# Encoder trunk on one core: later turns and two more products ahead of gate/up, grid transfers spread over attention units

## The chip, the cores and the metric

One Trainium2 chip, one NeuronCore of it. The metric is the device time of one execution in microseconds (us). The engines are named as the profile names them: PE is TensorE (PEld its weight loads), DVE VectorE, ACT ScalarE, POOL GpSimd, SP SyncE, which issues every DMA of this kernel; "SPq" is its queue.

## What is computed

Two transformer layers on 1024 tokens of width 1024, all float32. Layer 0 mixes tokens by windowed attention (12 heads, window of 128 to each side, T5 bias, sink), layer 1 by attention over a 16 x 64 grid of tokens (8 x 16 neighbourhood, relative bias). Four heads of each layer attend to a memory of 256 rows. Then a SwiGLU feed-forward layer:

```python
h = rms_norm(x, norm_mix_pre[i])
tok = windowed_gqa(...) if i % 2 == 0 else neighbourhood_attn(...)
mixed = concatenate([tok, mem_out]) @ w_out[i]
x = x + rms_norm(mixed, norm_mix_post[i])
h = rms_norm(x, norm_ffn_pre[i])
gu = h @ w_gu[i]                      # 1024 x 5632
f = (silu(gu[:, :2816]) * gu[:, 2816:]) @ w_down[i]
x = x + rms_norm(f, norm_ffn_post[i])
```

## The kernel before

**Products of float32.** Each operand is split into a high part (`fp32r`, ScalarE, L115, L918 or L1063) and a low part (the difference, VectorE or POOL, L116, L920 or L1064). A product is three matmuls: high x high, low x high, high x low (`mm3`, L91 to L93).

**Attention of a layer** (`heads`) runs over eight groups: six pairs of heads (0 to 5) and two pairs of memory heads (6, 7), in the order 0, 6, 1, 7, 2, 3, 4, 5. A group has 16 units (eight blocks of 128 query rows by two heads). For each unit PE computes scores (L254, L255), transposes probabilities (L282) three units later and weighs values (L292) five units later; between these the projection of the next group's queries is fed in evenly. Queries come in two halves of 512 columns. Where the two heads aren't set apart by the engines, `q_tiles` makes the high part (L208) and the low part (L209, `ql`) and three DMA moves (L201) put them into place; PE needs the moves of a half before the half's first scores.

**The grid bias of layer 1** is prepared in layer 0's attention by DMAs alone (`grid_tables`): 8 transfers fill two tables in DRAM from masks, 16 and 16 copy rows of the bias (rpb_d), and 16 and 8 copy from those to `bias_d`, all issued at L372. They are five lists; `group(p).units()` of a windowed pair takes one list and issues it in full, so the pairs 0, 1, 2, 3, 4 have them (L734). `keep_in_program_order` pins each issue behind what was emitted just before it on SP's queue.

**The output projection** runs over eight tiles of 128 tokens. After the matmuls of tile i, tile i - 1 is turned: `turn_tile` transposes its normed rows on PE (L186), ScalarE copies them to `z` (L838) and splits some into B11, B21, B22 (L97, L98). `tail` is the norm of a tile: two squares on ScalarE (L431), `ms` on VectorE (L161), `r` by POOL's power (L165), the scaling (L436), the sum with x (L437), a second square (L176), `ms` (L163), `r` again, and `ht` (L178), which the turn reads. From tile 4 on `combine` makes four differences (L853) on POOL, those of the last on VectorE, which are the operands T1 to T4.

**Gate/up** is a Strassen-Winograd product of 2 x 2 blocks: 22 iterations, f = 0, 11, 1, 12, ..., each of seven products of twelve matmuls (`product`). `A11 x B11` and `A12 x B21` need only tiles 0 to 3; the other five need T2, T1, T3, T4 and B22 and so all tiles, with the weight sums S1 to S4 (`Sums`, L954 to L957) and A22, split by `piece` (`gh` on ScalarE, `gl` on VectorE). Ahead of the T blocks the kernel computes the two products of gates 0, FH (11) and 1; the third gate's two stay in PSUM (`kept`) until iteration 2. Raw weights pass through a ring of two slots (`wr`), split gates through one of three (`wh`, `wl`).

**What sets the order.** Within attention PE's order is the program's. Elsewhere a planner places each instruction on its engine's queue by its own estimates of when it is ready, with the program's order as priority; engines then work their queues in order. `high_priority(offset=-60)` puts the query splits and moves 60 places back.

Of the kernel before, what the change touches and what calls it, by code (L numbers as in the profile page):

```python
# [66 lines left out]
def build(nc, tc, ctx, x_in, mem_in, wts, t5, onehot, sinks, rpb, maskb, gains, out):  # L67
# [43 lines left out]
    low = [nc.gpsimd]  # L111

    def split_raw(u, raw, pl, n, tiles=None, pin=False):
        h, lo = tiles or unit_tiles(u, pl, n)
        a = nc.scalar.activation(h, raw, AF.Copy)  # L115
        b = low[0].tensor_tensor(lo, raw, h.bitcast(F32), ALU.subtract)  # L116
        if pin:
            tc.keep_in_program_order(a)
            tc.keep_in_program_order(b)
        return h, lo  # L120
# [52 lines left out]
    def norm_rows(npool, xt, g, nb):  # L173
# [4 lines left out]
        nc.vector.scalar_tensor_tensor(ht, xt, r, g, ALU.mult, ALU.mult)  # L178
        return ht

# [59 lines left out]
    class Unit:  # L240


        def __init__(self, pair, j, hh, lo, nk, bias, sink, k):
            self.pair, self.j, self.hh, self.lo, self.nk = pair, j, hh, lo, nk
            self.bias, self.sink, self.k = bias, sink, k

# [54 lines left out]
    def heads(at2, groups):  # L301
# [29 lines left out]
        for units, its in groups:  # L331
# [3 lines left out]
            for n, u in enumerate(units):  # L335
                for part in range(2):
                    if part == 0:
                        u.scores(at2)
# [281 lines left out]
    for layer in range(DEPTH):  # L620
# [86 lines left out]
        if windowed:  # L707
# [12 lines left out]

            def group(p, order=order):
# [9 lines left out]
                def units():  # L731
                    if p < 5:
                        bias_tiles(p + 1)
                    for step in grid_todo.pop(0) if grid_todo else []:  # L734
                        step()
                    if p == order[2]:
                        mem_back(1)
                    return units_of(pr, bias, PAIRS_A[p])
# [45 lines left out]
        for m in range(2):  # L784
            pr = pair_of(6 + m, lambda m=m: mks[m], lambda b: mvs[b], 2 * m)
            units_by[6 + m] = lambda pr=pr: units_of(pr, None, None)
# [108 lines left out]
        for i in range(NT):  # L895
# [11 lines left out]
            if prev is not None:  # L907
                turn_tile(i - 1, prev)
            prev = tail(npool, i, accs, gpost, gpre, xt, x_new, False, 3)
# [5 lines left out]

        def piece(src):
# [3 lines left out]
            nc.vector.tensor_tensor(lo, src, h.bitcast(F32), ALU.subtract)  # L920
            return h, lo

        def product(A, B):
            acc = psO.tile([P, HALF], F32, name="acc", tag="acc")
# [115 lines left out]
        A = Sums(0, gates[0], spare.pop, nc.gpsimd)  # L1040
        gates.append(gate_unit(FH))
        for gate in gates:
# [6 lines left out]
        gates.append(gate_unit(1))  # L1049
        A11, A12 = ([t[:, k * HALF:(k + 1) * HALF] for t in gates[2][1]] for k in range(2))  # L1050
        kept = [product(A11, B11), product(A12, B21)]
        A.all()
        turn_tile(NT - 1, prev)
# [3 lines left out]
        T2, T1, T3, T4 = (block(cB, f"T{k}") for k in (2, 1, 3, 4))  # L1057
# [9 lines left out]
        for n in range(NF):  # L1067
            f = n // 2 + n % 2 * FH
            if n:
                gate = gates[n] if n < 3 else gate_unit(f)  # L1070
                if n == 2:
# [4 lines left out]
            else:  # L1076
                p1 = c11 = tmp("e")
                nc.scalar.activation(p1, kept.pop(0) if n == 2 else product(A.A11, B11), AF.Copy)
            act_sums(f, *gate_up(f, A, p1, c11, kept.pop(0) if n == 2 else None))
# [250 lines left out]
```

## Time and profile before

| | us |
|---|---|
| median of 3 runs (2249.93 to 2253.44) | 2252.22 |
| the profiled execution | 2251.45 |
| its span, first to last instruction | 2249.6 |
| PE busy in the span | 2143.0 |
| DVE busy | 1511.8 |
| ACT busy | 1063.4 |
| POOL busy | 718.9 |

Mean granted clock of PE over the span: 0.983. PE's matmuls are pipelined, so its busy time overlaps from one to the next. Layer 0's attention ends near 350 us, its projection near 448; gate/up of layer 0 follows until some 900 us, the down projection until some 1128; layer 1 repeats this, with its projection ending near 1574.

### The profile page before, as it was taken

To read this page: it belongs to the slowest core of one execution; us is meant where nothing else is said; L and a number is where in the kernel's file an instruction comes from. 1 tells how busy PE (TensorE), PEld (TensorE's weight loads), DVE (VectorE), ACT (ScalarE), POOL (GpSimd) and SP (SyncE) were. 2 spreads that over 40 slices of the span, in tenths; PEclk is the share of its full clock that TensorE was granted. 3 is DMA by queue.
4 is the path that set the end of the run, shared out by engine and by line. 5 is a ranking of instruction groups with operands and counts; after the bars stand their busy time and mean duration, and the time that the engine had idled before them with its cause. 6 is when DMAs were issued, how large, how long until landed. Compare 5 with 4: busy or idle time off the path is not lost.

```text
span 2249.6 us, 31265 instructions
## 1 busy us (share of the span) xinstructions
PE 2143.0 (95%) x10538; PEld 1781.7 (79%) x10538; DVE 1511.8 (67%) x2637; ACT 1063.4 (47%) x2162; POOL 718.9 (32%) x806
## 2 busy tenths in 40 slices
PE   7899898989999999999999999999899999999997
PEld 7678787768888888887788899778688888887875
DVE  5578785588777775557757665765887777755555
ACT  5488785453233332534457665754423333324333
POOL 3167661424333231102215342524233333310011
PEclk9999999999999999999999999999999999999999
DMA  6433445325555543866433222432245555437664
GB/s 207 119 87 94 126 145 148 108 75 178 183 178 173 176 157 122 286 200 225 149 107 97 78 78 74 137 113 102 74 176 184 179 174 174 163 118 276 197 200 146
DMA packets 153335, 336.49 MB, mean 150 GB/s; under 512 B 24759, under 2 KB 47159, under 8 KB 153176
## 3 DMA queue, kind: packets, MB, share of 16 engines
q1 hardware_dynamic: 153176, 334.50, 46.5%
q8 instruction: 84, 1.38, 0.3%
q14 instruction: 75, 0.61, 0.1%
HBM read 229.06 MB, written 95.03 MB: 144 GB/s over the span
## 4 chain that ended last, share of the span: by engine, by line
PE 72%; DVE 6%; ACT 5%; issue 5%; DMA 4%; POOL 3%; SPq 1%; POOLq 0%; DVEq 0%; ACTq 0%
PE acc L92 18%; PE acc L91 18%; PE acc L93 18%; PE psg L91 3%; PE psg L92 3%; PE psg L93 3%; PE psv L292 2%; PE pst L282 2%; PE pss L254 1%; PE pss L255 1%; POOL zh L853 1%; ACT sn L272 1%; DMA draw<-both_d 1%; DMA wr<-in_wts 1%; DMA draw<-in_wts 1%
## 5 line engine op out<-in xcount | busy, mean ns | idle before, releaser
L975 DVE TENSOR_TENSOR zt<-acc,zt 128x512 f32<-128x512 f32 x300 | 204.8, 686 | 155.4 <-PE acc L93 153.8
L274 POOL TENSOR_TENSOR sn<-sn,st 128x384 f32<-128x384 f32 (+1 forms) x256 | 188.2, 736 | 253.6 <-DVE st L273 219.1
L1120 DVE TENSOR_TENSOR dl<-draw,dh 128x1024 fp32r<-128x1024 f32 x119 | 148.5, 1257 | 133.6 <-ACT dh L1118 133.1
L1118 ACT ACTIVATE dh<-draw 128x1024 fp32r<-128x1024 f32 x119 | 125.3, 1058 | 172.9 <-PE acc L93 101.7
L92 PE MATMUL acc<-dl,dh 128*128 128x512 f32 x476 | 187.4, 394 | 8.8 <-DVE dl L1120 8.6
L91 PE MATMUL acc<-dh 128*128 128x512 f32 x476 | 186.2, 391 | 0.5 <-ACT dh L1118 0.5
L918 ACT ACTIVATE gh<-zt 128x512 fp32r<-128x512 f32 x168 | 104.4, 628 | 174.2 <-PE acc L92 155.4
L93 PE MATMUL acc<-dh,dl 128*128 128x512 f32 x476 | 185.9, 391 | 0.0
L994 POOL TENSOR_TENSOR tw<-tw 128x512 f32<-128x512 f32 x88 | 131.8, 1498 | 120.3 <-DMA tw<-in_wts 115.1
L116 DVE TENSOR_TENSOR wl<-wr,wh 128x1024 fp32r<-128x1024 f32 x92 | 120.1, 1306 | 68.5 <-ACT wh L115 66.9
L994 POOL TENSOR_TENSOR zt<-zt 128x512 f32<-128x512 f32 x66 | 90.4, 1370 | 205.1 <-DVE zt L972 201.6
L971 ACT ACTIVATE zt<-zt 128x512 f32<-128x512 f32 x84 | 53.1, 632 | 217.5 <-DVE zt L975 217.5
L91 PE MATMUL psg<-hH,wh 128*128 128x512 f32 x384 | 153.5, 400 | 1.8 <-DVE k L229 1.4
L115 ACT ACTIVATE wh<-wr 128x1024 fp32r<-128x1024 f32 x100 | 105.5, 1055 | 100.6 <-DMA wr<-in_wts 79.8
L92 PE MATMUL psg<-hL,wh 128*128 128x512 f32 x384 | 152.9, 398 | 0.0
L93 PE MATMUL psg<-hH,wl 128*128 128x512 f32 x384 | 152.7, 398 | 0.0
L1175 POOL TENSOR_TENSOR tt<-tt,g 128x512 f32<-128x512 f32 x28 | 45.8, 1652 | 334.3 <-ACT junk L1174 334.3
L292 PE MATMUL psv<-PT,v 128*128 128x256 f32 x656 | 143.1, 319 | 4.6 <-DVE attn L667 3.2
L98 DVE TENSOR_TENSOR PT<-pst,PT 128x384 fp32r<-128x384 f32 (+1 forms) x256 | 126.6, 495 | 29.2 <-ACT PT L97 24.6
L272 ACT ACTIVATE sn<-sn,st 128x385 f32<-128x385 f32 (+3 forms) x192 | 112.9, 588 | 61.8 <-DVE st L269 57.2
L920 DVE TENSOR_TENSOR gl<-zt,gh 128x512 fp32r<-128x512 f32 x168 | 129.6, 773 | 7.8 <-ACT gh L918 7.8
L282 PE MATMUL pst<-ident,sn 128*128 128x128 f32 x656 | 116.2, 277 | 8.2 <-POOL sn L274 4.5
(233 smaller groups left out, 6146.5 us busy)
## 6 DMA issues: line engine op xcount, KB each, us to landing
wr<-in_wts SPq DMA_DIRECT2D x146, 512.0 KB
draw<-both_d SPq DMA_DIRECT2D x88, 512.0 KB
both_d<-zt SPq DMA_DIRECT2D x88, 256.0 KB
tw<-in_wts SPq DMA_DIRECT2D x44, 512.0 KB
both_d<-tw SPq DMA_DIRECT2D x44, 512.0 KB
act_d<-zt SPq DMA_DIRECT2D x66, 256.0 KB
draw<-act_d SPq DMA_DIRECT2D x66, 256.0 KB
draw<-in_wts SPq DMA_DIRECT2D x66, 256.0 KB
```

The lines of the kernel that those rows point to most:

```text
L91: nc.tensor.matmul(ps, lh, rh, start=start, stop=False)
L92: nc.tensor.matmul(ps, lh, rl, start=False, stop=False)
L93: nc.tensor.matmul(ps, ll, rh, start=False, stop=stop)
L98: nc.vector.tensor_tensor(ol, ps, oh.bitcast(F32), ALU.subtract)
L272: nc.scalar.activation(sn[:, :m], sn[:, :m], AF.Exp, bias=nm, scale=-1.0, accum_out=ssum)
L274: nc.gpsimd.tensor_tensor(sf, sf, rinv.broadcast_to([P, n]), ALU.mult)
L282: nc.tensor.transpose(pt[:, c], self.sn[:, c * P:(c + 1) * P], ident)
L292: nc.tensor.matmul(pv[:, j % 2], pair.v(self.lo + c)[:, pair.vh + hh], self.PT[:, c], start=c == 0, stop=c == nk - 1)
L920: nc.vector.tensor_tensor(lo, src, h.bitcast(F32), ALU.subtract)
L975: nc.vector.tensor_tensor(o, a, b, ALU.add)
L994: nc.gpsimd.tensor_tensor(o, a, b, ALU.subtract)
L1120: eng.tensor_tensor(lo, raw, h.bitcast(F32), ALU.subtract)
```

## The change

In layer 0's attention each list of grid transfers is taken by a group, memory groups too, so the groups 0, 6, 1, 7, 2 have them; the n-th of its transfers is issued at the start of unit 1 + 14 n / length. Ahead of gate/up, tile 6 is turned after gate 0's two products and tile 7 after gate FH's two; the weight sums of f = 0 are made on VectorE in place of POOL, A22 is split at once, and the low parts of the other four sums are queued behind the last norm's `ht` and gate 1's low part (`late`). The products of gate FH + 1 are computed ahead as well, into the two PSUM banks of the turns, and used in iteration 3, for which the raw gate weights are loaded again. The T blocks are laid out in the reverse order. The diff:

```diff
@@ -109,11 +109,12 @@
         return [pl.tile([P, 1024], F32R, name=f"w{k}{u}", tag=f"w{k}{tag}", bufs=n) for k in "hl"]
 
     low = [nc.gpsimd]
+    split = [None]
 
     def split_raw(u, raw, pl, n, tiles=None, pin=False):
         h, lo = tiles or unit_tiles(u, pl, n)
         a = nc.scalar.activation(h, raw, AF.Copy)
-        b = low[0].tensor_tensor(lo, raw, h.bitcast(F32), ALU.subtract)
+        b = split[0] = low[0].tensor_tensor(lo, raw, h.bitcast(F32), ALU.subtract)
         if pin:
             tc.keep_in_program_order(a)
             tc.keep_in_program_order(b)
@@ -175,8 +176,15 @@
         ss = npool.tile([P, 1], F32, name="ss", bufs=4)
         nc.scalar.activation(ht, xt, AF.Square, scale=ROOT, accum_out=ss)
         r = rms(npool, [ss])
-        nc.vector.scalar_tensor_tensor(ht, xt, r, g, ALU.mult, ALU.mult)
+        normed[0] = nc.vector.scalar_tensor_tensor(ht, xt, r, g, ALU.mult, ALU.mult)
         return ht
+
+    normed = [None]
+
+    def behind(ins, first):
+
+        tc.add_manual_dep(ins.ins, first.ins.name, mybir.DependencyInfo(
+            mybir.DependencyClass.NoSync, mybir.DependencyReason.DATA), reason="queued behind")
 
     def turn(pspool, tag, ht, put):
 
@@ -243,6 +251,7 @@
         def __init__(self, pair, j, hh, lo, nk, bias, sink, k):
             self.pair, self.j, self.hh, self.lo, self.nk = pair, j, hh, lo, nk
             self.bias, self.sink, self.k = bias, sink, k
+            self.begin = []
 
         def scores(self, at2):
             j, hh, nk = self.j, self.hh, self.nk
@@ -335,6 +344,8 @@
             for n, u in enumerate(units):
                 for part in range(2):
                     if part == 0:
+                        for step in u.begin:
+                            step()
                         u.scores(at2)
                         line.append(u)
                     else:
@@ -718,6 +729,12 @@
                 for hh in range(2):
                     biases[p, hh] = b[:, hh]
 
+            def with_steps(us):
+                steps = grid_todo.pop(0) if grid_todo else []
+                for n, step in enumerate(steps):
+                    us[1 + n * (len(us) - 2) // len(steps)].begin.append(step)
+                return us
+
             def group(p, order=order):
                 c = p // 3
                 pr = pair_of(p, lambda: kts[c], lambda b: vts[b], 2 * c)
@@ -731,11 +748,10 @@
                 def units():
                     if p < 5:
                         bias_tiles(p + 1)
-                    for step in grid_todo.pop(0) if grid_todo else []:
-                        step()
                     if p == order[2]:
                         mem_back(1)
-                    return units_of(pr, bias, PAIRS_A[p])
+                    us = units_of(pr, bias, PAIRS_A[p])
+                    return with_steps(us)
 
                 return units, [q_item(U_A + p, keep_q(p), p in (order[0], order[7]))]
 
@@ -783,7 +799,7 @@
             units_by[p], needs[p] = group(p)
         for m in range(2):
             pr = pair_of(6 + m, lambda m=m: mks[m], lambda b: mvs[b], 2 * m)
-            units_by[6 + m] = lambda pr=pr: units_of(pr, None, None)
+            units_by[6 + m] = lambda pr=pr, then=with_steps if windowed else list: then(units_of(pr, None, None))
             needs[6 + m] = [q_item(um + m, keep_q(6 + m), not windowed)]
         for it in needs[order[0]]:
             now(it)
@@ -904,24 +920,29 @@
                         ds = slice(dh * HALF, (dh + 1) * HALF)
                         mm3(accs[dh], aH[:, c], aL[:, c], h[:, ds], lo[:, ds],
                             c0 + c == 0, c0 + c == 7)
-            if prev is not None:
+            if prev is not None and i < NT - 1:
                 turn_tile(i - 1, prev)
-            prev = tail(npool, i, accs, gpost, gpre, xt, x_new, False, 3)
+            before, prev = prev, tail(npool, i, accs, gpost, gpre, xt, x_new, False, 3)
         oph.close()
 
 
         gph = Phase()
         gp = gph.open(sb(f"gu{layer}", side="left"))
+
+        late = []
 
         def piece(src):
             h = gp.tile([P, HALF], F32R, name="gh", tag="gh", bufs=5)
             nc.scalar.activation(h, src, AF.Copy)
             lo = gp.tile([P, HALF], F32R, name="gl", tag="gl", bufs=5)
-            nc.vector.tensor_tensor(lo, src, h.bitcast(F32), ALU.subtract)
+            b = nc.vector.tensor_tensor(lo, src, h.bitcast(F32), ALU.subtract)
+            for ins in late:
+                behind(b, ins)
             return h, lo
 
-        def product(A, B):
-            acc = psO.tile([P, HALF], F32, name="acc", tag="acc")
+        def product(A, B, acc=None):
+            if acc is None:
+                acc = psO.tile([P, HALF], F32, name="acc", tag="acc")
             for kc in range(4):
                 ks = slice(kc * P, (kc + 1) * P)
                 mm3(acc, A[0][:, ks], A[1][:, ks], B[0][:, kc], B[1][:, kc], kc == 0, kc == 3)
@@ -1037,24 +1058,39 @@
         spare = [stage.tile([P, S], F32, name="attn", tag="attn", bufs=2) for _ in range(2)]
         spare = [t[:, k * HALF:(k + 1) * HALF] for t in spare for k in range(2)]
         gates = [gate_unit(0)]
-        A = Sums(0, gates[0], spare.pop, nc.gpsimd)
+        A = Sums(0, gates[0], spare.pop, nc.vector)
+        A.A22
         gates.append(gate_unit(FH))
-        for gate in gates:
+        for gate in gates[:]:
             p1 = gp.tile([P, D], F32, name="p1", tag="tw", bufs=2)
             p1, c11 = p1[:, :HALF], p1[:, HALF:]
             A11, A12 = ([t[:, k * HALF:(k + 1) * HALF] for t in gate[1]] for k in range(2))
             nc.scalar.activation(p1, product(A11, B11), AF.Copy)
             add(c11, product(A12, B21), p1)
             ahead.append((p1, c11))
-        gates.append(gate_unit(1))
-        A11, A12 = ([t[:, k * HALF:(k + 1) * HALF] for t in gates[2][1]] for k in range(2))
-        kept = [product(A11, B11), product(A12, B21)]
-        A.all()
-        turn_tile(NT - 1, prev)
+            turn_tile(NT - 3 + len(ahead), before if len(ahead) == 1 else prev)
+            if len(ahead) == 1:
+                gates.append(gate_unit(1))
+                late[:] = normed[0], split[0]
+                A.all()
+                late.clear()
+
+        def first_two(f, make):
+            if f != 1:
+                gates.append(gate_unit(f))
+            A11, A12 = ([t[:, k * HALF:(k + 1) * HALF] for t in gates[-1][1]] for k in range(2))
+            kept.append([make(A11, B11), make(A12, B21)])
+
+        def turned_bank():
+            return psT.tile([P, 4, P], F32, name="pst", tag="pst").rearrange("p k t -> p (k t)")
+
+        kept = []
+        first_two(1, product)
+        first_two(FH + 1, lambda A, B: product(A, B, turned_bank()))
         nph.close()
         stage_ph.close()
         cB = com_ph.open(sb(f"comB{layer}", side="right"))
-        T2, T1, T3, T4 = (block(cB, f"T{k}") for k in (2, 1, 3, 4))
+        T4, T3, T1, T2 = (block(cB, f"T{k}") for k in (4, 3, 1, 2))
         for n, ((tH, tL), (b, t)) in enumerate(((T2, (1, 1)), (T1, (0, 0)), (T3, (0, 1)), (T4, (1, 0)))):
             for i in range(4):
                 eng = nc.gpsimd if (n, i) in TPOOL else nc.vector
@@ -1067,16 +1103,17 @@
         for n in range(NF):
             f = n // 2 + n % 2 * FH
             if n:
-                gate = gates[n] if n < 3 else gate_unit(f)
-                if n == 2:
+                gate = gates[n] if n < 4 else gate_unit(f)
+                if n in (2, 3):
                     gate = load_raw(U_GU + 44 * layer + 2 * f), gate[1]
                 A = Sums(f, gate, lambda: tmp("s"), nc.vector)
             if n < 2:
                 p1, c11 = ahead[n]
             else:
                 p1 = c11 = tmp("e")
-                nc.scalar.activation(p1, kept.pop(0) if n == 2 else product(A.A11, B11), AF.Copy)
-            act_sums(f, *gate_up(f, A, p1, c11, kept.pop(0) if n == 2 else None))
+                two = kept.pop(0) if kept else [product(A.A11, B11), None]
+                nc.scalar.activation(p1, two[0], AF.Copy)
+            act_sums(f, *gate_up(f, A, p1, c11, None if n < 2 else two[1]))
             if n and summed < FH and summed * (NF - LEAD) <= (n - 1) * FH:
                 weight_sums(summed)
                 summed += 1
```

## Rows read from the trace of the kernel before

**Rows 1.** The page's first part: busy time, share of the span, instructions of each engine.
```profile
PE 2143.0 (95%) x10538; PEld 1781.7 (79%) x10538; DVE 1511.8 (67%) x2637; ACT 1063.4 (47%) x2162; POOL 718.9 (32%) x806
```
**Rows 2.** Windows: length, then PE PEld DVE ACT POOL busy, PEclk, DMA share, GB/s.
```profile
245.00:330.00 85.00, 72.13 (x442) 63.53 (x441) 61.74 (x190) 63.68 (x173) 51.57 (x99) 0.92 0.50 150
```
**Rows 3.** Timeline of SyncE's queue, layer 0's attention: start, length, what.
```profile
244.16 12.71 SPq L372 DMA_DIRECT2D bias_d<-rpb_d  x16
256.98 0.52 SPq L201 DMA_DIRECT2D q<-q  x1
...
280.85 6.22 SPq L372 DMA_DIRECT2D bias_d<-rpb_d  x8
```
**Rows 4.** Timelines of VectorE and of PE, layer 0's attention (idle before in brackets).
```profile
246.40 0.69 DVE L209 SCALAR_TENSOR_TENSOR ql<-psg,q 128x512 fp32r<-128x512 f32 x1
...
262.00 0.66 PE L254 MATMUL pss<-k,q 128*128 128x384 f32 x1 [6.98 <-DMA q<-ql]
```
**Rows 5.** Windows of the two idle stretches and of what follows each.
```profile
254.96:262.00 7.04, 0.06 (x1) 0.03 (x1) 1.64 (x5) 1.73 (x6) 2.03 (x4) 0.71 0.79 218
262.00:268.38 6.38, 6.38 (x22) 5.59 (x23) 3.14 (x9) 2.85 (x8) 1.10 (x3) 0.52 0.97 293
292.11:295.79 3.68, 0.01 (x2) 0.03 (x1) 2.77 (x6) 2.30 (x6) 1.97 (x4) 0.96 0.79 231
295.79:299.03 3.24, 3.24 (x12) 2.84 (x12) 0.87 (x4) 0.96 (x3) 0.39 (x1) 0.52 0.37 139
```
**Rows 6.** Timeline of PE, layer 0, from the projection's end to the T2 product.
```profile
449.73 1.06 PE L186 MATMUL pst<-ident,ht 128*128 128x128 f32 x8 [1.89 <-DVE ht L178]
...
453.40 0.39 PE L91 MATMUL acc<-B21H,wh 128*128 128x512 f32 x1
...
456.12 0.39 PE L91 MATMUL acc<-B11H,wh 128*128 128x512 f32 x1
...
463.79 0.52 PE L186 MATMUL pst<-ident,ht 128*128 128x128 f32 x3 [2.06 <-DVE ht L178]
466.39 0.80 PE L91 MATMUL acc<-B11H,wh 128*128 128x512 f32 x1 [2.08 <-ACT wh L115]
...
478.34 0.76 PE L92 MATMUL acc<-T2L,gh 128*128 128x512 f32 x1 [3.94 <-DVE T2L L1064]
```
**Rows 7.** Windows of that passage in layer 0, the product after it, layer 1's passage.
```profile
447.85:478.34 30.49, 20.53 (x90) 16.45 (x90) 24.20 (x25) 20.74 (x38) 14.63 (x11) 0.91 0.21 68
478.34:483.16 4.82, 4.82 (x11) 3.76 (x12) 4.82 (x9) 1.33 (x4) 0.00 (x0) 0.50 0.02 3
1573.73:1603.71 29.98, 20.68 (x90) 16.45 (x90) 24.19 (x25) 20.73 (x38) 14.65 (x11) 0.93 0.23 71
```
**Rows 8.** Timeline of ScalarE, the same passage of layer 0.
```profile
450.48 1.06 ACT L115 ACTIVATE wh<-wr 128x1024 fp32r<-128x1024 f32 x1 [4.92 <-DMA wr<-in_wts]
```
**Rows 9.** Timeline of VectorE, the same passage of layer 0.
```profile
440.70 1.41 DVE L436 SCALAR_TENSOR_TENSOR tt<-acc,r,g 128x512 f32<-128x512 f32 x2 [3.20 <-POOL r L165]
...
457.16 1.78 DVE L920 TENSOR_TENSOR gl<-wr,gh 128x512 fp32r<-128x512 f32 x1
...
461.17 0.14 DVE L163 TENSOR_SCALAR ms<-ss 128x1 f32<-128x1 f32 x1
...
462.36 1.29 DVE L178 SCALAR_TENSOR_TENSOR ht<-xt,r,g 128x1024 f32<-128x1024 f32 x1 [0.45 <-POOL r L165]
...
469.34 0.69 DVE L853 TENSOR_TENSOR zh<-zh 128x512 f32<-128x512 f32 x1 [1.75 <-ACT zh L838]
...
476.43 1.76 DVE L1064 TENSOR_TENSOR T2L<-zh,T2H 128x512 fp32r<-128x512 f32 x1
```
**Rows 10.** Timeline of SyncE's queue, the same passage of layer 0.
```profile
446.69 0.33 SPq L105 DMA_DIRECT2D wr<-in_wts  x1
```
**Rows 11.** Windows, iteration 2 of gate/up in layer 0.
```profile
506.00:520.00 14.00, 14.00 (x62) 11.27 (x61) 13.80 (x19) 5.36 (x9) 4.53 (x3) 1.00 0.41 141
```
**Rows 12.** Timeline of GpSimd (POOL), the passage of layer 0.
```profile
453.48 6.62 POOL L853 TENSOR_TENSOR zh<-zh 128x512 f32<-128x512 f32 x4
```

## The prediction

> **What bounds the kernel now.** I read the page's first part, then the stages, then TensorE's gaps. TensorE (PE) is busy for 95% of a span of 2249.6 us [rows 1], so only time in which it stands still, or runs at its lower clock, can be won. The windows show where that is: from 245 to 330 us, in the first layer's attention, PE is busy for only 72.13 of 85 us, at a granted clock of 0.92 [rows 2]. The changed attention code acts there; the rest of the change acts on the passage from the output projection to gate/up, which runs once per layer.
>
> *Attention.* SyncE's queue shows 16 transfers rpb_d to bias_d issued in one run, 12.71 us from 244.16, and right behind them, at 256.98, the first of three moves that put a query half into place [rows 3]. PE needs that half: it stood idle 6.98 us until the last move, q<-ql, had landed [rows 4]. Its low part had been made by 246.40 + 0.69 = 247.1 [rows 4], so it is the queue that was late. The same pattern returns with 8 transfers at 280.85 [rows 3]. The windows price both [rows 5]: 7.04 us idle, then 6.38 us at clock 0.52, which cost 6.38 x 0.48 = 3.1; then 3.68 idle and 3.24 x 0.48 = 1.6. Together **15.4 us**. The lower clock (1.2 of 2.4 GHz) follows PE's idle time in both cases.
>
> *Into gate/up.* PE's timeline [rows 6] gives the order: tile 7's projection ends at 449.73 - 1.89 = 447.84; then the turn of tile 6 (idle 1.89 for its norm), four products, the turn of tile 7 (idle 2.06), two products (idle 2.08 for their weights), then the first product with T2 (idle 3.94 for T2's low part). From 453.40 to 456.12 one whole product passes: 2.72 us at the full clock. Eight transposes take 1.06 at most. The work between 447.84 and 478.34 is then 6 x 2.72 + 2 x 1.06 = 18.4 us, and the window is 30.49 long [rows 7]: 12.1 lost. The remaining 11 matmuls of the T2 product run at clock 0.50 for 4.82 us [rows 7], 2.3 more than 11/12 of 2.72. So 14.4 us in layer 0. Layer 1's window is 29.98 [rows 7], which by the same sums loses 13.9. Together **28.3 us**.
>
> **The change, part by part.**
>
> *Grid transfers.* Number and issue time stay: 32 + 24 + 8 issues, the 16 above at 12.71/16 = 0.79 us. What moves is their place: the five lists go to the first five groups in the order 0, 6, 1, 7, 2, and within a group to units 1 to 14. Each is pinned behind the queue's previously emitted instruction, so the query moves of a half now stand behind a few transfers, not behind 16. A half was ready at 247.1 and wanted at 254.96: 7.9 us of slack, of which the run of 16 used 256.98 - 247.1 = 9.9 before the first move left; three or four transfers use 3. Pairs 3 and 4 carry none at all afterwards. The bytes are the same: the DMA share was 0.97 while the 16 drained [rows 5], and fourteen units' time in place of 12.71 us lowers that. The moves q<-q of pairs 7 and 2 get slower neighbours; that cost is bounded by nothing and by the 15.4 themselves. I take **14 us** saved.
>
> *Ring order on the queue.* Each later weight load or store of attention results waits behind at most a few 0.79 us issues instead of a run; nothing on it is needed within that time, so 0.
>
> *Turns later, two products more.* Turn 6 now follows gate 0's products, turn 7 those of gate FH, then four products stand ahead of T2 instead of none. Counted from the end of tile 7's projection, at full clock: two products to 5.4; turn to 6.5; two to 11.9; turn to 13.0; four to 23.9; then T2. What is ready when?
> - Tile 6's norm ended about 1.9 after that point [rows 6]: covered by the 5.4 of gate 0.
> - Tile 7's norm. ScalarE sat 4.92 us waiting for gate FH's load [rows 8], with tile 7's squares behind it, until about 451.5, that is 3.7 late. That load had waited for VectorE, which had waited 3.20 for POOL's r, which stood behind the four weight sums on POOL [rows 9]. The sums now go to VectorE, into just that idle time, so the load leaves earlier and part of the 3.7 goes. Then, on VectorE, the row of ms (461.17) stood behind low parts of the weight sums that began at 457.16 [rows 9]; `late` puts these behind the norm. The norm ended at 462.36 + 1.29 = 463.65 [rows 9], 15.8 after the end of the projection. Without the low parts (about 2.8) it is 13.0; without the late load as well, 9.4. It is needed at 11.9: a wait between 0 and 1.1, I take 0.7.
> - Gate 1's load takes the ring slot that A22's low part frees, made at 457.16 + 1.78 = 458.94 [rows 9]. `A.A22` is now asked for directly after the sums, so it leaves some 5 us sooner and is in time for 13.0.
> - Gate FH + 1's load can leave only when gate 1's low part is made, near 11.5; a load took from 446.69 [rows 10] to 450.48 [rows 8], 3.8 us, the split another 1.06 + 1.2. That is 17.6 against 18.4 needed, with nothing to spare: 0 to 3 us, I take 1.
> - T2. With T1 and T2 laid into the space of the projection's weights, their first three quarters no longer wait for tile 7. After turn 7 remain two copies, four differences, one split: about 5 us, against 10.9 of products. What may be late is VectorE, which has three low parts of gates, four of sums, the differences and the T splits to do in these 24 us. I take 2.
>
> So about 3.7 of the 12.1 remain, and no slow product, unless a gap near 4 comes back: 0.5.
>
> *What the two products uncover.* They are taken out of iteration 3 of gate/up, which then has five, 13.6 us, as 0 to 2 have. VectorE was busy for 13.80 of 14.00 us from 506 to 520 [rows 11], in iteration 2: it is the next bound and has one more short iteration to get through, besides an n = 0 that no longer runs at the half clock. Price: 0 to 4 us per layer, I take 1.3. The extra load of gate FH + 1's raw weights and the two PSUM banks held longer: 0 (no turn uses those banks later, and the load is issued iterations ahead), at the worst one load, 3.8 us; below 0 is excluded, since both only add.
>
> Residual per layer 3.7 + 0.5 + 1.3 = 5.5, so 14.4 - 5.5 = 8.9 and 13.9 - 5.5 = 8.4, **17.3 us** for both.
>
> *One meeting of engines, weighed.* A difference on VectorE took 0.69 us with POOL idle (469.34), a T2 split 1.76 with POOL at work (476.43) [rows 9]: 1.07 dearer. POOL's four differences of a turn, 6.62 us from 453.48 [rows 12], now fall later, beside the second half of tile 7's norm. If all four hit it, turn 7 comes 4.3 us later.
>
> The Trainium skill, SBUF — State Buffer, section "Who interferes with whom", says that a VectorE instruction with two SBUF inputs and a GpSimd one that reads SBUF exclude each other, the later waiting for the whole of the earlier. By that rule all four meetings cost, and the sum of both layers would be 17.3 - 8.6 = 8.7 rather than 17.3. The trace agrees in size (1.07 us beside POOL instructions of 1.3 to 2.2), but where the instructions meet it can't tell.
>
> **Sum.** 14 + 17.3 = 31.3 us. The profiled execution took 2251.45 us, so 2220.2; the median shown stands 0.8 above it: **2221 us**.
>
> **Rivals.**
>
> *A. VectorE is the bound after all.* Its 13.80 of 14.00 [rows 11] and the dearer meetings [rows 9, 12] speak for it; against it, that VectorE itself stood idle 3.20 us for POOL's r [rows 9]. Each layer then keeps only 4 us or so: 14 + 8.7 = 22.7, 2230 us.
>
> *B. The attention stalls move.* The 16 transfers now run in pair 7 and the 8 big ones in pair 2; if their traffic alone, not the issue, made q<-q late, the idle time comes back there: 0 + 17.3, 2235 us. For it: 0.97 DMA share [rows 5]. Against: the first move was only issued at 256.98 [rows 3].
>
> *C. The order on PE doesn't change as the text says.* A planner sets it by its own estimates of when things are ready; if it lets the turns keep their place, or puts the last products behind T2, only attention gains: 2238 us.
>
> *D. Slower.* A transfer pinned behind a query move or a store that waits holds the whole queue; where that happens in each of the five groups, a query half is late five times instead of twice. Price 7.0 + 3.1 = 10.1 each: 50.5 - 15.4 = 35 lost against 17.3 won, 2270 us. It decides from when three moves are issued more than 8 us late in a group. The queue's rows show runs, but no such wait between pinned ones.
>
> **How the numbers follow.** Forecast 0.48 (alone 2211 to 2229), A 0.18, B 0.12, C 0.10, D 0.06; B and C together, which leaves about nothing, 0.06. The low end takes both stalls and all but the two layers' last 0.7 us each: 2252.2 - 15.4 - 26.9 = 2210, and 2 more for what I didn't see: 2208. The high end takes in B and C: 2239. A difference under 0.2%, 4.5 us, is what a measurement of this kernel can't tell from none. Faster: forecast, A, B, C: 0.88. Same: 0.06. Slower: D, 0.06.
>
> **What the profile of after would show.** Right: no idle PE over 1 us between 245 and 310 that ends on q<-ql, and the clock at 1.00 there; SyncE's rpb_d and bias_d issues in runs of a few, ended by the third windowed pair; turn 6 after two products and turn 7 after four; four products between turn 7 and T2; POOL without weight sums ahead of gate/up; ms ahead of the low parts. Wrong: the same 7 us idle in the second memory group (B), the order of before (C), PE waiting for VectorE's gl in iterations 1 to 3 (A), or a wait at gate FH + 1's wh longer than 3 us, which would mean that the two-slot ring, not the norm, sets this passage.

## The result and the profile after

The changed kernel takes 2230.83 us (median of 4 runs, 2228.48 to 2233.92) beside 2251.07 us of the kernel before on the same chip: ratio 0.9916, 95% interval 0.9904 to 0.9929. It is 0.8% faster. The forecast was 2221 us with a range of 2208 to 2239: right in direction and within the range, 10 us too good. The profiled execution took 2229.09 us.

The page of the kernel after, its span and busy times, which answer to [rows 1]; PE is busy for 9 us less, the span is 22 us shorter:

```profile
span 2227.3 us, 31239 instructions
PE 2133.9 (96%) x10538; PEld 1772.9 (80%) x10538; DVE 1514.2 (68%) x2645; ACT 1060.9 (48%) x2162; POOL 715.3 (32%) x798
```

Where the 22.3 us of span came from is read from the starts of the same landmarks in PE's timeline of both kernels:

| stretch | before | after | gained | forecast |
|---|---|---|---|---|
| start to layer 0's projection | 350.71 | 344.75 | 6.0 | 14 |
| from there to layer 1's first scores | 812.2 | 805.0 | 7.2 | 8.9 |
| layer 1's attention | 313.8 | 313.3 | 0.5 | 0 |
| from layer 1's projection to the end | 772.9 | 764.3 | 8.6 | 8.4 |

The passage into gate/up gave nearly what it was to give; attention gave less than half. The waits of PE from 100 to 300 us, by what ended them (us in total, times, longest), first before, then after:

```profile
PE pss L254 <- DMA q<-ql: 10.7, 2, 7.0
PE pss L254 <- ACT sn L262: 4.0, 4, 2.2
PE pss L254 <- DVE st L269: 2.5, 4, 1.4
PE psg L91 <- DVE k L229: 1.4, 1, 1.4
PE pst L282 <- DVE PT L98: 0.7, 1, 0.7
```

```profile
PE pss L263 <- DVE st L278: 6.6, 5, 2.1
PE pst L291 <- DVE PT L98: 2.6, 4, 1.1
PE pss L263 <- ACT sn L271: 1.9, 3, 1.1
PE psg L91 <- DVE k L237: 1.4, 1, 1.4
PE psv L301 <- DVE pa L678: 1.1, 3, 0.5
PE pss L263 <- DMA q<-ql: 1.0, 1, 1.0
PE pst L291 <- POOL sn L276: 0.7, 1, 0.7
PE psv L301 <- DVE st L282: 0.6, 1, 0.6
```

The 10.7 us of waits on the query moves [rows 4] are down to 1.0, and the granted clock of 254 to 296 us is 1.00, where it had dropped to the lower level [rows 5]. SyncE still issues the transfers in runs of up to eight (6.21 us from 206.63), but no query move stands right behind one of these. But new waits stand there, above all of scores on VectorE's bias-and-maximum step (`st`, L278). Followed by the same PE instruction, the changed kernel is 3.6 us ahead at 142 us, 6.9 us **behind** at 250, and 6.1 ahead at 299 (times of the kernel before): the two old stalls gave 13 us, and 10.5 were lost ahead of them. One of the two new waits over 2 us, on PE, and what VectorE did just before it (timelines of the kernel after):

```profile
235.37 0.44 PE L263 MATMUL pss<-k,q 128*128 128x384 f32 x1 [2.02 <-DVE st L278]
```

```profile
232.82 1.36 DVE L117 TENSOR_TENSOR wl<-wr,wh 128x1024 fp32r<-128x1024 f32 x1 [0.54 <-DMA bias_d<-rpb_d]
234.11 0.68 DVE L217 SCALAR_TENSOR_TENSOR ql<-psg,q 128x512 fp32r<-128x512 f32 x1
234.71 0.60 DVE L278 CUSTOM_DVE_ANT_0 sn<-pss,bias,nsink_t 128x384 f32<-128x384 f32 x1
```

PE had filled both score banks by 232.7 and needed one emptied. The step that empties it stood in VectorE's queue behind the low part of a weight unit and the low part of a query half. The 0.54 us ahead of `wl` are put down to a grid transfer, but ScalarE made the high part that `wl` needs from 231.74 to 232.79, which covers them; the unit's own load had been issued at 214.40. PE's order in this stretch is the program's and has not changed; VectorE's was laid out anew by the planner.

In the passage PE waits neither for turn 6 nor for turn 7 nor for T2. One wait is left in each layer, at the low part of gate FH + 1 (PE's timeline; the pair in the other layer is 4.62 us at 1583.30), and behind it the granted clock is 0.50 for 4.9 us, from 465.57 to 470.43 (stretches: us, then busy time and count of each engine, granted clock, DMA share):

```profile
460.61 0.39 PE L92 MATMUL pst<-B11L,wh 128*128 128x512 f32 x1
465.57 0.80 PE L93 MATMUL pst<-B11H,wl 128*128 128x512 f32 x1 [4.58 <-DVE wl L117]
```

```profile
442.00:460.38 18.38, 18.38 (x90) 15.10 (x88) 14.93 (x17) 14.45 (x26) 8.31 (x7) 1.00 0.26 86
460.38:473.00 12.62, 8.04 (x25) 6.12 (x24) 12.52 (x15) 8.36 (x16) 6.78 (x4) 0.73 0.14 43
```

T2 starts at 473.02. At the full clock the 22 matmuls from 465.57 would have ended at 470.6, so wait and clock cost 4.6 + 2.4 = 7.0 us. VectorE meanwhile (its timeline):

```profile
440.26 1.28 DVE L179 SCALAR_TENSOR_TENSOR ht<-xt,r,g 128x1024 f32<-128x1024 f32 x1 [1.62 <-POOL r L166]
...
450.65 2.31 DVE L179 SCALAR_TENSOR_TENSOR ht<-xt,r,g 128x1024 f32<-128x1024 f32 x1
...
453.49 1.71 DVE L117 TENSOR_TENSOR wl<-wr,wh 128x1024 fp32r<-128x1024 f32 x1
455.13 4.68 DVE L938 TENSOR_TENSOR gl<-attn,gh 128x512 fp32r<-128x512 f32 x4
459.73 0.68 DVE L996 TENSOR_TENSOR p<-acc,p 128x512 f32<-128x512 f32 x1
460.33 2.35 DVE L869 TENSOR_TENSOR zh<-zh 128x512 f32<-128x512 f32 x2
462.61 0.68 DVE L98 TENSOR_TENSOR B22L<-pst,B22H 128x512 fp32r<-128x512 f32 x1
463.21 1.17 DVE L869 TENSOR_TENSOR zh<-zh 128x512 f32<-128x512 f32 x1
464.30 1.21 DVE L117 TENSOR_TENSOR wl<-wr,wh 128x1024 fp32r<-128x1024 f32 x1
465.44 0.68 DVE L869 TENSOR_TENSOR zh<-zh 128x512 f32<-128x512 f32 x1
```

and GpSimd beside it:

```profile
450.59 7.47 POOL L869 TENSOR_TENSOR zh<-zh 128x512 f32<-128x512 f32 x4
460.37 3.46 POOL L1100 TENSOR_TENSOR T2L<-zh,T2H 128x512 fp32r<-128x512 f32 x2 [2.31 <-ACT T2H L1099]
```

ScalarE began the high part of that unit at 458.71 and ended it at 459.8; `wl` began 4.5 us later. The four late low parts (`gl`) were just done by then; a sum (`p`), three differences (`zh`) and the low part of B22, which stood behind them in the queue, came first.

### The profile page after: what moved, and what is told of

It is laid out like the page before. It is cut to its first block, busy times and chain, and to the rows that moved or that the text cites. A ratio compares the mean times of both kernels' runs of the same rounds, so it can differ in the third digit from the quotient of the medians.

```text
span 2227.3 us, 31239 instructions
## 1 busy us (share of the span) xinstructions
PE 2133.9 (96%) x10538; PEld 1772.9 (80%) x10538; DVE 1514.2 (68%) x2645; ACT 1060.9 (48%) x2162; POOL 715.3 (32%) x798
```

## The experiments

All are edits of the changed kernel, but for e1. Ratios are to the kernel before on the same chip (2248.49 to 2251.07 us). "Projection" is the start of layer 0's output projection in the profiled execution, "to layer 1" the time from there to layer 1's first scores, "end" that from layer 1's projection to the end.

| kernel | us | ratio to before (95%) | projection | to layer 1 | end |
|---|---|---|---|---|---|
| before | 2251.07 | 1 | 350.71 | 812.2 | 772.9 |
| changed | 2230.83 | 0.9916 (0.9904 to 0.9929) | 344.75 | 805.0 | 764.3 |
| changed, again | 2230.78 | 0.9921 (0.9906 to 0.9936) | 345.29 | 803.8 | 765.2 |
| e1 spread alone | 2244.71 | 0.9985 (0.9976 to 0.9994) | 347.84 | 809.3 | 771.2 |
| e2 passage alone | 2235.95 | 0.9943 (0.9929 to 0.9958) | 350.73 | 806.2 | 764.7 |
| e3 no grid | 2220.25 | 0.9877 (0.9861 to 0.9894) | 331.95 | 805.9 | 765.3 |
| e4 low part first | 2226.57 | 0.9902 (0.9887 to 0.9917) | 348.21 | 802.0 | 761.2 |
| e5 bias first | 2239.11 | 0.9950 (0.9932 to 0.9968) | 351.58 | 806.4 | 765.6 |
| e6 one head | 2223.65 (1 run) | | 339.02 | 803.5 | 765.2 |
| e7 second half | 2227.89 | 0.9907 (0.9890 to 0.9924) | 343.60 | 804.9 | 764.3 |
| e8 in gate/up | 2273.68 | 1.0101 (1.0077 to 1.0124) | 332.98 | 861.3 | 765.6 |
| e9 turns only | 2233.48 | 0.9928 (0.9911 to 0.9945) | 344.81 | 806.0 | 766.0 |
| e10 both | 2219.58 | 0.9868 (0.9853 to 0.9882) | 341.73 | 802.6 | 760.3 |
| e12 behind loads | 2242.97 | 0.9975 (0.9966 to 0.9984) | 333.50 | 831.0 | 760.5 |

Where the expectations count 56 grid transfers, it is 64 (8 fills, 32 and 24 copies).

**The two parts alone.** e1 puts the hunks on `begin` and `with_steps` into the kernel before; e2 takes them out of the changed one:

```diff
+                    for step in grid_todo.pop(0) if grid_todo else []:
+                        step()
                     if p == order[2]:
                         mem_back(1)
-                    us = units_of(pr, bias, PAIRS_A[p])
-                    return with_steps(us)
+                    return units_of(pr, bias, PAIRS_A[p])
...
```

> Part alone: the grid transfers are spread, the passage into gate/up stays as it was before. If the two parts are independent, attention of layer 0 ends as in the changed kernel: first matmul of the output projection at 344.7 us (350.71 before), and the time is about 2251 - 6.5 = 2244.5 us. My forecast of 14 us for this part would want 336.7 us and 2237. If the passage helped through something in attention (no mechanism known), the projection starts elsewhere than 344.7.

> Part alone: the later turns, the two more products and the late low parts, with the grid transfers in bursts as before. Independent parts: projection starts at 350.7 us, layer 0's passage is 7.3 us shorter and layer 1's 8.6, together about 2251 - 16 = 2235 us, and TensorE's wait before the rest of gate FH+1's first product is 4.6 us in both layers. If the passage's gain needs the shifted phase of the first part, less than 16.

They add up: 0.15% and 0.57% make 0.72% of the 0.8%, within the intervals. Most of the gain is the passage, 12.5 us on that chip; the spread alone is worth 3 to 4 us. e1's projection came 3 us later than expected, and most of that is the wait told of under the hardware below (PE 2.98 us, 0.51 in the changed kernel). The wait at gate FH + 1 is there in e2 too (4.61 and 4.57 us).

**No grid transfers.** Layer 1's bias tables are neither prepared nor read.

```diff
-    grid_todo = grid_tables()
+    grid_todo = []
...
-                    dma.dma_start(out=b, in_=bias_d[PAIRS_B[p][hh]])
+                    dma.dma_start(out=b, in_=wts[0][:, :640].rearrange("p (c k) -> p c k", k=P))
```

> The 56 grid transfers (fills, bias copies, table copies) are left out of the changed kernel, and layer 1 reads weights in the place of its bias tables, so its result is another one. Theory T (the new waits of pairs 1 and 2 come from the transfers: they hold SyncE's queue and the DMA engines, and weights and q moves land late): the 10 us come back, projection at 334 to 337 us, total about 2221. Theory V (they come from the order in which VectorE's queue was laid out: weight splits and query low parts ahead of bias-and-maximum steps that are ready): taking the transfers out at run time gives little, projection still at 341 to 346 us, with waits of scores on VectorE's bias step of several us; the layout may move them to other places.

Projection at 331.95, 12.8 us earlier: in amount this is theory T. But the planner laid VectorE's queue out anew here as well, and this run can't tell the two causes apart. What left PE's waits of 100 to 300 us are above all those on VectorE, 6.6 us on the bias step being 2.1 here (the four largest):

```profile
PE pss L263 <- ACT sn L271: 2.7, 4, 1.0
PE pss L263 <- DVE st L278: 2.1, 3, 1.4
PE psg L91 <- DVE k L237: 1.4, 1, 1.4
PE psv L301 <- ACT PT L97: 0.6, 1, 0.6
```

**One head of twelve.** All 64 transfers in their units, with a twelfth of the data; eleven heads' tables stay unprepared and layer 1 reads weights, as in e3. One of the three edits:

```diff
-                steps[-1].append(go(rpb_d[k][:, r, ds, rs:rs + 8], rpb[:, ds, 15 - r + rs:23 - r + rs]))
+                steps[-1].append(go(rpb_d[k][:1, r, ds, rs:rs + 8], rpb[:1, ds, 15 - r + rs:23 - r + rs]))
...
```

> The same 56 transfers at the same units of the same pairs, each for one head of twelve, so with a twelfth of the data (eleven heads' tables stay unprepared; layer 1 reads weights in their place). The order of VectorE's queue stays that of the changed kernel from pair 2 on, and becomes that of the kernel without transfers in pairs 0 and 1. Theory T: with little to move and short issues on SyncE, projection starts near 332 to 335 us. Theory V: what is gained is gained in pairs 0, 1 and the second memory pair, up to some 240 us, and nothing behind it where the order is the same; projection at 335 to 341 us.

Projection at 339.02, as V had it. Against the same instructions of the changed kernel PE is 1.5 us behind at 142 us and 3.67 ahead at 218.6. From there to 232.5 the difference is constant, 3.65 to 3.68: VectorE has the same order in both, and the data, copies of 288 KB in the one and 24 KB in the other, make no difference that shows; but only two of them are issued in that stretch. Then it jumps to 5.56 us at the score shown above. VectorE at that place in e6:

```profile
228.56 0.67 DVE L217 SCALAR_TENSOR_TENSOR ql<-psg,q 128x512 fp32r<-128x512 f32 x1
229.15 0.60 DVE L278 CUSTOM_DVE_ANT_0 sn<-pss,bias,nsink_t 128x384 f32<-128x384 f32 x1
```

The query's low part is there, the `wl` is not: its 0.54 + 1.36 = 1.90 us are the 1.88 that PE gains. Behind 240 us no grid transfer is left, and the difference stays within 0.5 us of 5.86. So of 7.4 us between 142 and 246, 1.9 are the order's; the 5.2 up to 218.6, where data differ and, up to 210, the order too, this run leaves open.

Beside e3, e6 says more. At 213 us PE is 0.4 us behind e3, at 233 us 4.2, and at the projection 7.1, and VectorE's order differs between the two. With a twelfth of the data in e6, these 7 us aren't the data's. For the last 2.8 of them, behind e6's last grid transfer (issued at 232.84), VectorE's order is what is left; for the 3.8 ahead of it the issues on SyncE's queue are not ruled out.

**Another order, all the data.** Same pairs, but units 8 to 14 instead of 1 to 14:

```diff
-                    us[1 + n * (len(us) - 2) // len(steps)].begin.append(step)
+                    us[len(us) // 2 + n * (len(us) // 2 - 1) // len(steps)].begin.append(step)
```

> The changed kernel with the same 56 transfers, in full and in the same five pairs, but spread over the second half of each pair's units (8 to 14) instead of units 1 to 14. That alone gives VectorE another order: as in the kernel without transfers in pair 0, the second memory pair and pair 2, another one in the first memory pair and pair 1. Theory V (order decides): most of the 10 us come back with every byte still moved; no waits over 1 us of scores on the bias step in the second memory pair and pair 2; projection at 334 to 341 us, total 2220 to 2227. Theory T (the transfers at run time decide): closer together they cost as much or more, projection at 344 us or later.

By 246 us PE is 5.2 us ahead of the changed kernel, with every byte moved, though at other times. In the second memory pair and pair 2 no scores wait over 1 us on the bias step any more; in pair 1, where the order is not that of e3, 2.32 us of it stand at 165.11. The transfers have their share too, as theory T had it: standing closer together, they make query moves late (waits of PE, 100 to 300 us):

```profile
PE pss L263 <- DMA q<-ql: 4.7, 3, 2.3
PE pss L263 <- DVE st L278: 4.4, 4, 2.3
PE pss L263 <- ACT sn L271: 2.4, 3, 1.1
```

Of the 10.2 us between the changed kernel and e3 at 246 us, 5.2 come back here; of the 4.7 us of waits on moves, 3.4 stand ahead of 246 and are most of the rest. The profiled run then lost 3.3 us at 317 to a wait told of under the hardware below, so the projection came at 343.60, later than expected; the times (0.9907 beside 0.9921 on the same chip) are too near to tell it from the changed kernel.

**Preferring the bias step.** The planner was to take layer 0's bias steps ahead of what is ready at the same time:

```diff
-                nc.vector.tensor_tensor_reduce(
...
+                with tc.high_priority(offset=40 if self.sink is not None else 0):
+                    nc.vector.tensor_tensor_reduce(
...
```

> All transfers of the changed kernel stay where they are; only the planner is told to prefer layer 0's bias-and-maximum steps on VectorE over low parts that are ready at the same time. Theory V (the order of VectorE's queue is what the new 10 us are): the five waits of scores on the bias step (6.6 us in sum) fall under 3 us and the projection starts 3 to 6 us earlier than the 347.8 to 348.2 us of the last two runs. Theory T (the transfers themselves, at run time): projection within 1.5 us of that. If low parts of weights then come late instead, the waits reappear before projections' products (psg on wl) and nothing is gained.

A miss. The waits stayed (6.3 us in four), those of PE on the low parts of probabilities rose to 8.9 us up to 345 (3.8 in the changed kernel run again), and the projection came at 351.58. Why the priority did not help is argued, not shown: it decides only between steps that the planner believes ready, and the low parts ahead of the bias step it would have believed ready earlier. The run speaks neither for V nor for T.

**Gate FH + 1's low part first.**

```diff
                 gates.append(gate_unit(1))
+                gates.append(gate_unit(FH + 1))
                 late[:] = normed[0], split[0]
...
-            if f != 1:
-                gates.append(gate_unit(f))
-            A11, A12 = ([t[:, k * HALF:(k + 1) * HALF] for t in gates[-1][1]] for k in range(2))
+            A11, A12 = ([t[:, k * HALF:(k + 1) * HALF] for t in gates[2 + len(kept)][1]] for k in range(2))
```

> Gate FH+1 is loaded and split ahead of the late low parts of unit 0's sums in program order, so that VectorE's queue has its low part (wl) ahead of those four. Theory Q (the 4.6 us wait of TensorE in each passage is VectorE's queue): wl starts at about 460 instead of 464.3, the wait falls to 0.5 us or less, the half-clock stretch behind it goes; the first wait left is T2's low parts, about 2 us; gain 3 to 6 us a layer, total 2219 to 2225. Rival (the two-slot ring sets it: the load lands too late): wl waits on its load, gain under 1.5 us a layer, total 2228 to 2231.

Theory Q. Counted from tile 7's turn, which is 2.88 us later here (456.74 beside 453.86), `wl` starts 4.5 us sooner, while ScalarE begins the high part at the same place (4.85 us behind the turn in both). The clock stays at 1.00, and what is left of the waits is small (PE's timeline):

```profile
463.96 0.50 PE L93 MATMUL pst<-B11H,wl 128*128 128x512 f32 x1 [0.25 <-DVE wl L117]
466.97 0.50 PE L91 MATMUL pst<-B21H,wh 128*128 128x512 f32 x1 [0.45 <-DVE B22L L98]
471.85 0.47 PE L92 MATMUL acc<-T2L,gh 128*128 128x512 f32 x1 [1.61 <-DVE T2L L1099]
```

The stretches behind the projections are 802.0 and 761.2 us; the seven profiles with the changed passage as it was (changed twice, e2, e3, e5, e6, e7) have 803.5 to 806.4 and 764.3 to 765.6. Against their means of 805.1 and 764.9 us, 3.1 and 3.7 are won, at the low end of what was expected; this run's projection came late, at 348.21. The time alone does not tell e4 from the changed kernel (0.9902 beside 0.9916 and 0.9921, overlapping intervals); e10 below does. What `wl` waits for now is the load: ScalarE waits 3.12 us for it (2.54 in the changed kernel), VectorE 0.68 for ScalarE.

**Later turns without the two products.**

```diff
-        first_two(FH + 1, lambda A, B: product(A, B, turned_bank()))
...
-                gate = gates[n] if n < 4 else gate_unit(f)
-                if n in (2, 3):
+                gate = gates[n] if n < 3 else gate_unit(f)
+                if n == 2:
```

> The passage with the later turns, the late low parts and gate 1's two products, but without the two of gate FH+1, which are made in their own iteration as before. My forecast gave them the place of the wait for T2's low parts. Theory P (they fill a hole): TensorE ends gate 1's products at about 460 and T2's low parts are ready at 467 to 469, so a wait of 7 to 9 us at T2 in place of 4.6 us plus 5.5 us of useful products: 3 to 5 us a layer worse than the changed kernel with its 4.6 us wait, total 2236 to 2241. Rival (without gate FH+1's load and low part on VectorE the low parts of T2 come sooner by the 1.3 us of wl, and the wait is no longer than before): within 3 us of the changed kernel.

The rival: 0.9928 beside 0.9921 for the changed kernel. T2 starts at 465.40 after 5.28 us of waiting, and the products are made later:

```profile
459.73 0.39 PE L93 MATMUL acc<-B21H,wl 128*128 128x512 f32 x1
465.40 0.79 PE L91 MATMUL acc<-T2H,gh 128*128 128x512 f32 x1 [5.28 <-ACT T2H L1098]
```

As built, the two products of gate FH + 1 fill the hole and dig another of nearly the same size: they are worth 1 to 2 us in all, less than a measurement tells. The later turns, with the sums and low parts moved along, are the gain.

**The transfers out of attention.** e8 issues three at the end of each of layer 0's 22 iterations of gate/up; e12 issues them at the start of the iterations and queues each behind the weight load issued last instead, unpinned (and has e4's edit).

```diff
+            for step in grid_later[:3]:
+                step()
+            del grid_later[:3]
             if n and summed < FH and summed * (NF - LEAD) <= (n - 1) * FH:
```

> All 56 transfers in full, taken out of attention and issued three by three at the end of the 22 iterations of layer 0's gate/up. Attention of layer 0 then has the instruction order of the kernel without them. Expected: projection at 332 to 335 us as in the run without transfers, and SyncE and the DMA engines have room in gate/up (15 us an iteration, three issues of about 0.8 us): total within 3 us of that run's 2220. Rival: SyncE's queue in gate/up holds gate and up loads behind transfers that wait on each other, TensorE waits for weights, and half or more of the 12 us is given back (2225 to 2231).

> As in the run with the transfers in gate/up, three an iteration of layer 0, but each is queued right behind the weight load issued last, not behind the stores of the sums, and gate FH+1's low part goes first. If what lost that run its time was SyncE's queue (loads of gate and up held behind transfers that were themselves held behind stores), the waits of TensorE on weights in gate/up (17.2 and 6.6 us) fall under 3 us in sum: attention as without transfers (projection at 332 to 334 us), total 2212 to 2219, below the 2219.6 us of the best so far. Rival (64 more issues of some 0.7 us are too many for SyncE's queue in this stage, wherever they stand): waits of 5 us and more remain, total above 2225.

Attention was as forecast (332.98 and 333.50), gate/up was not: 56 and, with e4's 3 us counted, 29 us lost. In e8 the pinned transfers stand behind stores that wait for sums, and the loads behind both; the largest wait (SyncE's and PE's timelines):

```profile
518.88 3.00 SPq L1036 DMA_DIRECT2D both_d<-zt  x3
522.90 0.32 SPq L1036 DMA_DIRECT2D act_d<-zt  x1
523.27 2.35 SPq L383 DMA_DIRECT2D rpb_d<-in_rpb  x3
525.67 1.01 SPq L1021 DMA_DIRECT2D tw<-in_wts  x2
526.73 0.90 SPq L105 DMA_DIRECT2D wr<-in_wts  x2
```

```profile
533.90 0.79 PE L91 MATMUL acc<-B11H,wh 128*128 128x512 f32 x1 [17.16 <-ACT wh L116]
```

In e12 that wait is gone and PE is busy throughout from 600 to 800 us, but the last iterations, where bias_d is copied, wait 4.4, 3.2 and 10.0 us for weights, and 800 to 1000 us has a clock of 0.93: in amount this is the rival. Why those loads are late there was not followed up.

**Both improvements.** The edits of e7 and e4 together, with the changed kernel on the same chip:

> The two improvements together: transfers in the second half of the units, and gate FH+1's low part ahead of the late low parts. They lie in stages that share nothing, so they add up: projection as in the run with the second half alone, 3 us less in each layer's stretch from projection to the end of gate/up, total 5 to 7 us below that run; below the changed kernel by 8 to 14 us.

> The changed kernel as it is, on the chip of the two above, so that they can be compared with it directly. 0.992 of the time before; if its projection starts at 347 to 348 us here (and not at 344.7), the 3 us between are a difference from run to run that every run of it carries at random, at the write of the memory projection ahead of a bias step near 320 us.

2219.58 us, 0.9868 of before, and 11.2 us below the changed kernel; the intervals lie apart. It is the best version that was run. Against e7, from which it differs by e4's edit alone, on the same chip, it is 8.3 us faster with intervals apart: 1.9 us up to the projection, where e7 had its late wait, and 2.3 and 4.0 behind the two projections. So e4's gain is in the time as well. The changed kernel's projection at 345.29 says that the 3 us lost in e1, e4 and e7 are not in every run.

## Why the prediction was right or wrong

- **Passage, 17.3 us: right in size** (7.2 + 8.6 = 15.8), by other terms than summed, so in part by luck. Norm of tile 7: taken 0.7, is 0; PE waits for neither turn. T2: taken 2, is 0. VectorE-bound iterations: taken 1.3, is 0, as from T2's start to 560 us PE has no wait at all. Gate FH + 1: taken 1, with an end at 3, and 0.5 for a slow product; it is 4.6 and 2.4 of clock, so 7.0 against a whole residual of 5.5. The step that failed there is the one on gate FH + 1: its load left right behind gate 1's low part and came within 3.5 us, about as priced (3.8), but the low part was taken to follow at once, and the queue of VectorE, in which `wl` stands behind what `late` had put back, had no term. e4 leaves the load and the high part where they were and moves `wl` ahead in that queue, and the wait falls to 0.25 us. My test, a wait over 3 us at that gate's `wh` as a sign of the ring, did not catch it: PE took `wh` without waiting (460.38) and stood at `wl`.
- **POOL beside VectorE: the meetings came, at another place.** VectorE worked almost without a gap from 450.65 up to `wl`, and beside POOL's work six of its steps took longer: `ht` of tile 7 2.31 us (tile 6's 1.28), gate 1's `wl` 1.71 (later 1.21), two late low parts 1.78 each (0.68), two differences 1.57 and 1.17 (0.68). That is 5.1 us in sum, as much as the wait of 4.58 us, so without the meetings `wl` would have been nearly in time: an estimate from these rows, as no run takes POOL out of the stretch. e4 shows that the order alone is enough to end the wait. Turn 7, on whose way the prediction weighed the meetings, was not held, as PE had products until 453.86. By the rule of the Trainium skill, SBUF — State Buffer, "Who interferes with whom", I had the passage at 8.7 us; it is 15.8, because the terms above came out at 0. The rule itself agrees with the rows.
- **Attention, 14 us: wrong in size.** Both old stalls and their clock went, worth 13 us, as the steps said. What failed is the step "nothing on it is needed within that time, so 0", with the taking of 14 where late neighbours were bounded by nothing and 15.4: I took VectorE's order as given. With the transfers spread over the units of five groups, weight and query low parts stand between scores and their bias step, and 10.5 us were lost ahead of the old stalls. The order is shown as the cause for the 1.9 us of one place (e6) and for 2.8 us behind the last transfer (e6 beside e3); in e7 another order, with the transfers at other times, gave back 5.2 in sum. How the rest divides between order, issues and late moves stays open, and that the planner's estimate of when weights land made the order is argued from its working, not shown.
- **The number.** 2230.83 lies in the range because the range took in rivals that cost 14 us and more; the forecast of 31.3 us was half as much again as the 20.2 measured, and 8 us of the excess are attention's.
- **Rivals.** A's time (2230) came out, but not by A: VectorE's queue holds PE once in the passage, and nowhere in the iterations. B and D: 1.0 us is left on the query moves, in one place. C: the turns stand where the text puts them.

## What to carry to other kernels

A moved transfer moves more than itself: where a planner orders the queues by estimated landings, compare the order of every engine's queue before pricing the move, and look for long steps (weight splits) that now stand ahead of a step that frees a bank. Work put ahead to fill a hole is worth only what its own inputs allow; follow its last input through the queue of the engine that makes it. When two late steps compete for one engine, put first the one whose reader runs out of other work.

## Of the hardware, not expected

The same low part on VectorE with and without POOL's differences beside it (one line's instructions, min/median/max ns, first in the changed kernel, then in e4, where VectorE makes them after POOL has ended):

```profile
L938 DVE TENSOR_TENSOR gl<-attn,gh x4: 677/1228/1777, 455.1 to 459.1; 128x512 fp32r<-128x512 f32 x4
```

```profile
L938 DVE TENSOR_TENSOR gl<-attn,gh x4: 684/686/689, 463.8 to 465.6; 128x512 fp32r<-128x512 f32 x4
```

And runs of one order of instructions differ by 3 us at one place: near 318 us POOL needs a buffer that a store of the memory projection still reads, and the store held POOL up for 1.39 us in the changed kernel and for 3.43 in e4, whose attention has the same order on VectorE (POOL's timeline):

```profile
318.75 0.18 POOL L276 COPY sn<-nsink_t 128x1 f32<-128x1 f32 x1 [1.39 <-DMA mem_scr<-sn]
```

```profile
320.44 0.18 POOL L276 COPY sn<-nsink_t 128x1 f32<-128x1 f32 x1 [3.43 <-DMA mem_scr<-sn]
```
